# A hybrid decoder trunk: the RWKV triangular solves' copies, stores and loads on other queues and at other steps, and the last key tile's products moved

## The chip, the cores and the metric

The kernel runs on one core of a Trainium2 chip. The metric is the device time of one execution in microseconds, the median of several runs.

## The reference

Two decoder layers over 1024 positions of width 1024. Layer 0 mixes tokens by a gated linear recurrence, layer 1 by RWKV-7 time mixing; each layer also has cross-attention into 256 memory tokens and a squared-ReLU MLP. The change touches the RWKV mixer alone:

```python
xx = x_prev - x
r = (x + xx*mu[0]) @ w_rkv[0];  k = (x + xx*mu[2]) @ w_rkv[1];  v = (x + xx*mu[3]) @ w_rkv[2]
...
state = state * w_t + sa * b_t + v_t * k_t          # sa = state @ a_t; a = -kk, b = kk * a
y_t = state @ r_t                                   # 16 heads of 64, 1024 steps
```

All arrays are float32. The kernel does the recurrence in 16 chunks of 64 positions. Within a chunk the state correction needs the inverse of a unit triangular 64x64 matrix for each head and chunk.

## The kernel before

A float32 product is done as three matmuls on a high and a low part (lines 304 to 306, in `mm3`); `split` (lines 203 and 204) makes the parts, the high one on ScalarE, the low one on VectorE. Almost all tiles are 128x1024 "units" from one pool of 45 buffers. Matmul weights are loaded on SyncE's DMA queue (line 235) in the order in which they are used, a few ahead.

The program text gives the instructions a priority; a planner with an engine model then fixes the order on each engine and hands out buffers as they come free in its plan. On the chip each engine works its list in that order. `with self.behind():` pins what is emitted in it behind the last instruction emitted so far on the same engine. `self.between` holds small pieces of work, one of which is emitted after each product of three matmuls in a tile's second half.

The RWKV stage has 20 steps, counted by `aside(step)`. In steps 0 to 6 the eight 128-column tiles f of the keys are multiplied (tiles 6 and 7 together in step 6); `prep_head(f)` empties the PSUM tile (lines 1183 and 1184) and `prep_rest(f)` makes kp (line 1190), the squares sq (line 1192), b and a (lines 1193 to 1197) and stores them. `sums` and `gram` of a tile follow a step or more later (lines 1218 to 1248) and store the chunks' triangular matrices. Steps 7 to 12 multiply the receptance (tiles 0 and 1 together, then 2 to 5, then 6 and 7 together; line 1353 empties them), steps 13 to 19 the values. Two PSUM tiles of this size are in use, so a product waits until the one before the last has been emptied.

The triangular matrices of two tiles f are inverted together as solve q: `solve_load` fetches them (line 1252) and sets the result tile to the identity (lines 1253 and 1254), `solve` does 31 pairs of a multiply (line 1268) and an add (line 1270), `solve_store` makes a transposed copy (line 1280) and stores both (lines 1281 and 1282). Solves 0 to 2 run on GpSimd, solve 3 on VectorE through `self.between`. The solve inverts 32x32 halves; `merge_load` (lines 1286 to 1294), `merge` (two small products, lines 1306 and 1313) and `merge_store` (line 1320) join them for each f. The steps at which load, solve and store of solve q stand are the lists

```python
SL, SO, ST = (2, 4, 6, 9), (2, 4, 6, 9), (2, 4, 6, 12)
```

and those of the merges are ML (9 + f), ME (10 + f) and MS (11 + f).

Of the kernel before, what the change touches and what calls it, by code (L numbers as in the profile page):

```python
# [992 lines left out]

TURNS = [[f] for f in range(6)] + [[6, 7]]

SL, SO, ST = (2, 4, 6, 9), (2, 4, 6, 9), (2, 4, 6, 12)
ML, ME, MS = range(9, 17), range(10, 18), range(11, 19)
SE = [lambda nc: nc.gpsimd] * 3 + [lambda nc: nc.vector]
DA = (2, 1)
LD = 6  # L1000
POST = lambda nc: nc.vector
# [47 lines left out]
def rwkv_make_mix(self, X, i, hf, out, js=range(KT // 2)):  # L1049

    nc = self.nc

    def parts(m):
        h, l = self.split(m)
        out.extend((h[:, s], l[:, s]) for s in (slice(0, 512), slice(512, 1024)))

    ms = []
    for j in js:
        m = self.unit()
        for k in (2 * j, 2 * j + 1):  # L1060
            o = (k % 2) * 512
            mu = self.col("mu", i * 8 + k)
            nc.scalar.activation(m[:, o:o + 512], X[hf][:, k, :], AF.Copy, scale=self.omu[:, i * 8 + k:i * 8 + k + 1])
            if hf:
                nc.scalar.activation(m[:, o:o + 1], X[0][:, k, 511:512], AF.Identity, scale=mu, bias=m[:, o:o + 1])
            nc.vector.scalar_tensor_tensor(m[:, o + 1:o + 512], X[hf][:, k, :511], mu, m[:, o + 1:o + 512], ALU.mult, ALU.add)
        ms.append(m)
        if len(ms) > 1:
            parts(ms.pop(0))
    parts(ms.pop(0))  # L1070
# [31 lines left out]
def rwkv(self, X, xt, lw_wa, lw_g, post):  # L1102
    nc, I = self.nc, self.I
# [3 lines left out]
    XTd = self.dram([128, 8, 1024])  # L1107
# [3 lines left out]
    Mod = self.dram([8, 2, 32, 16, 32])  # L1111
    Ld = self.dram([4, 2, 2, 2, 16, 32, 32])
    Xd = self.dram([4, 2, 2, 2, 16, 32, 32])
    Xnd = self.dram([8, 2, 16, 32, 32])
# [9 lines left out]
    for hf in range(2):  # L1124
# [13 lines left out]
        if hf:  # L1138
            h = maps[0][2]
# [4 lines left out]
    h = maps[1][2]  # L1144
# [11 lines left out]
    dk, st_k, mg, sol, ld, sm, xts = {}, {}, {}, {}, {}, {}, {}  # L1156
# [22 lines left out]
    def prep_head(f, pk):  # L1179
        a, P, IP = dk[f]  # L1180

        at = self.unit()
        nc.scalar.activation(at, pk, AF.Copy, scale=self.nkk[:, f:f + 1])
        nc.vector.tensor_mul(IP, IP, pk)  # L1184
        dk[f] = a, P, IP, at

    def prep_rest(f):
        a, P, IP, at = dk.pop(f)
        kp = self.unit()
        nc.vector.tensor_scalar(kp, a, self.col("k_a", f), self.kam[:, f:f + 1], ALU.mult, ALU.add)  # L1190
        sq = self.unit()
        nc.scalar.activation(sq, at, AF.Square)
        nc.vector.scalar_tensor_tensor(a, a, self.col("k_k", f), IP, ALU.mult, ALU.mult)

        nc.vector.tensor_mul(ch(at)[:, :, 1:], ch(at)[:, :, 1:], ch(P)[:, :, :63])
        nc.sync.dma_start(MVd[:, f, 0, :], at)
        nc.vector.tensor_mul(kp, kp, IP)
        for h in range(2):
            nc.sync.dma_start(STd[hr[h], f, h, :], a[hr[h], :])
            nc.sync.dma_start(STd[hr[h], f, 1 - h, :], kp[hr[h], :])  # L1200
        st_k[f] = sq, a, at

    def prep(f, pk):
        prep_head(f, pk)
        if f < 6:
            prep_rest(f)
        if f == 7:
            rwkv_make_mix(self, X, 0, 0, xr[0], range(2, 4))
            gram(5)
            rwkv_make_mix(self, X, 0, 1, xr[1])  # L1210
            prep_rest(6)
            prep_rest(7)

    def sums(f):

        ps = sm[f] = self.bank()
        for tt in range(8):
            self.between.append(lambda tt=tt: mm(ps[:, tt * 2:tt * 2 + 2], st_k[f][0][:, tt * 128:tt * 128 + 128], self.ind,
                                                 start=True, stop=True))

    def gram(f):
        sq, a, at = st_k.pop(f)
        ps = sm.pop(f)
        d2 = self.sp.tile([128, 16], F32, name=self.nm("d2"), tag="d2", bufs=3)
        nc.vector.tensor_scalar(d2.rearrange("p (h t) -> p h t", h=2), ps[:, 0:16].rearrange("p (t h) -> p h t", h=2), 1e-24, None, ALU.max)
        nc.vector.reciprocal(d2, d2)
        for par in range(2):
            for h in range(2):
                nc.sync.dma_start(self.db[h * 64:h * 64 + 64, f * 16 + par * 8:f * 16 + par * 8 + 8],
                                  d2[par * 64:par * 64 + 64, h * 8:h * 8 + 8])  # L1230
        mt = self.unit()
        dv = self.db[:, f * 16:f * 16 + 16].rearrange("p (a t) -> p t a", a=2)
        for e in range(2):
            pg = self.bank()
            for c in range(8):
                s = slice(c * 64, c * 64 + 64)
                sc = slice(e * 512 + c * 64, e * 512 + c * 64 + 64)
                for h in range(2):
                    rs = slice(h * 64, h * 64 + 64)
                    mm(pg[rs, s], a[rs, sc], at[rs, sc], start=True, stop=True)  # L1240
            nc.vector.tensor_tensor(mt[:, e * 512:e * 512 + 512].rearrange("p (t a i) -> p t a i", a=2, i=64),
                                    pg.rearrange("p (t a i) -> p t a i", a=2, i=64),
                                    dv[:, e * 4:e * 4 + 4].unsqueeze(3).broadcast_to([128, 4, 2, 64]), ALU.mult)
        for h in range(2):
            for b in range(2):
                rs = slice(h * 64 + b * 32, h * 64 + b * 32 + 32)
                nc.sync.dma_start(Ld[f // 2, b, f % 2, h].rearrange("c s t -> s c t"), ch(mt)[rs, :, b * 32:b * 32 + 32])
            nc.sync.dma_start(Mod[f, h], ch(mt)[h * 64:h * 64 + 32, :, 32:64])

    def solve_load(q):  # L1250
        sol[q] = L, xt_ = [self.unit() for _ in range(2)]
        (nc.sync if q == 3 else nc.gpsimd).dma_start(L, Ld[q].rearrange("b q h c s t -> (b q h c) (s t)"))
        nc.gpsimd.memset(xt_, 0.0)
        nc.gpsimd.memset(xt_[:, ::33], 1.0)

    def solve(q):

        L, xt_ = sol[q]
        eng = SE[q](nc)
        tmp = stmp[q == 3]  # L1260
# [16 lines left out]

    def solve_store(q):
        L, xt_ = sol.pop(q)
        SE[q](nc).tensor_copy(L[0:64].rearrange("p (s j) -> p s j", j=32), xt_[0:64].rearrange("p (j s) -> p s j", s=32))  # L1280
        nc.gpsimd.dma_start(Xd[q].rearrange("b q h c s t -> (b q h c) (s t)"), xt_)
        nc.gpsimd.dma_start(Xnd[2 * q:2 * q + 2].rearrange("q h c s t -> (q h c) (s t)"), L[0:64])

    def merge_load(f):
        XT = self.unit()
        nc.gpsimd.memset(XT, 0.0)
        XN = self.unit()
        xc = ch(XT)
        for h in range(2):
            for b in range(2):  # L1290
                rs = slice(h * 64 + b * 32, h * 64 + b * 32 + 32)
                nc.gpsimd.dma_start(xc[rs, :, b * 32:b * 32 + 32], Xd[f // 2, b, f % 2, h].rearrange("c s t -> s c t"))
            nc.gpsimd.dma_start(XN[h * 64:h * 64 + 32, 0:512].rearrange("p (c t) -> p c t", t=32), Xnd[f, h].rearrange("c s t -> s c t"))
            nc.gpsimd.dma_start(XN[h * 64:h * 64 + 32, 512:1024].rearrange("p (c t) -> p c t", t=32), Mod[f, h])
        mg[f] = XN, XT

    def merge(f):
        XN, XT = mg.pop(f)
        xc = ch(XT)
        r0 = [slice(h * 64, h * 64 + 32) for h in range(2)]  # L1300
# [14 lines left out]
        for h in range(2):  # L1315
            nc.scalar.copy(xc[r0[h], :, 32:64], ps[r0[h], :].rearrange("p (c t) -> p c t", t=32))
        xts[f] = XT

    def merge_store(f):
        nc.gpsimd.dma_start(XTd[:, f, :], xts.pop(f))  # L1320

    def aside(step):

# [5 lines left out]

    self.depth, self.ahead = DA  # L1330
    decay(0)
# [15 lines left out]
    def early(f):  # L1347
        ld[f] = self.unit()
        nc.sync.dma_start(ld[f], Pd[f * 128:f * 128 + 128, :])
# [6 lines left out]
    for i, fs in enumerate([[0, 1], [2], [3], [4], [5], [6, 7]]):  # L1356
        for f in fs:
            early(f)
        if i == 5:
            self.later.append(lambda: rwkv_make_mix(self, X, 3, 0, xv[0], range(3)))  # L1360
        if i in (1, 2):
            sums(5 + i)
        self.fphase(I["b_w_rkv"][0, 0], fs, xr, evac_r, spread=i == 0)
        if i in (1, 2):
            gram(5 + i)
        aside(len(TURNS) + i)
# [201 lines left out]
    for c in range(16):  # L1568
# [4 lines left out]
        s = cst[c]  # L1573
# [113 lines left out]
```

## Time and profile before

| | |
|---|---|
| median of three runs | 3032.07 us (3031.96 to 3038.93) |
| profiled execution | 3026.98 us; span of its instructions 3025.3 us |
| TensorE busy | 2866.9 us, 95% of the span |
| VectorE, ScalarE, GpSimd busy | 1799.5, 1350.1 and 1186.1 us |
| RWKV stage, key products to the last merge | about 1400 to 1810 us of the span |

The profiled execution is one of its own, some 5 us below the median of the runs. PE is TensorE's matmuls, DVE VectorE, ACT ScalarE, POOL GpSimd, SP SyncE (it only issues DMAs). A busy share is an average: what TensorE lacks is found in the stretches in which it is not busy, and in those in which the granted clock (PEclk, 1.00 is 2.4 GHz) is below one.

### The profile page before, as it was taken

What the parts mean: (1) busy time and instruction counts of PE and PEld (TensorE: products, weight loads), DVE (VectorE), ACT (ScalarE), POOL (GpSimd) and SP (SyncE); (2) the same over time, 40 slices, a digit from 0 to 9 for tenths busy, and PEclk for the clock granted to TensorE, in tenths of its full rate; (3) what the DMA queues carried; (4) which work ended last, traced back from release to release, by engine and by line L of the source; (5) the groups of instructions that cost most, each with busy time, mean ns of one, the idle gap of its engine ahead of it and who ended that gap; (6) DMA issues with size and microseconds to landing.
All of it is one profiled execution on the core that took longest, in us unless ns stands there. A gap on an engine that the chain in (4) does not pass through costs nothing. (4 is left out here: it accounts for less than half of the span.)

```text
span 3025.3 us, 42919 instructions
## 1 busy us (share of the span) xinstructions
PE 2866.9 (95%) x16987; PEld 2382.4 (79%) x16987; DVE 1799.5 (59%) x1991; ACT 1350.1 (45%) x1939; POOL 1186.1 (39%) x1108
## 2 busy tenths in 40 slices
PE   7999999898999999989978999999999899999998
PEld 6888898786888878877866777878888678887886
DVE  5576552547355688767673726884344644568776
ACT  5464342535454543447340534443244545454332
POOL 2000100015666754441587424652001466667442
PEclk9999999998999999999988999999999999999999
DMA  8213261122544564332646889852312244455443
GB/s 260 73 42 101 80 213 55 57 84 70 169 154 154 216 213 148 115 126 86 168 113 198 223 241 230 183 134 84 105 43 90 71 152 153 153 205 197 161 139 119
DMA packets 370857, 421.93 MB, mean 139 GB/s; under 512 B 78960, under 2 KB 280928, under 8 KB 370656
## 3 DMA queue, kind: packets, MB, share of 16 engines
q1 hardware_dynamic: 356128, 371.85, 40.9%
q0 software_dynamic: 14064, 46.75, 4.3%
q8 instruction: 134, 2.20, 0.3%
q14 instruction: 67, 0.55, 0.1%
q10 hardware_dynamic: 464, 0.59, 0.1%
HBM read 284.31 MB, written 134.74 MB: 139 GB/s over the span
## 5 line engine op out<-in xcount | busy, mean ns | idle before, releaser
L204 DVE TENSOR_TENSOR u<-u,u 128x1024 fp32r<-128x1024 f32 (+1 forms) x518 | 816.7, 1604 | 344.2 <-ACT u L203 328.6
L304 PE MATMUL p<-u,u 128*128 128x512 f32 (+1 forms) x1920 | 717.9, 377 | 44.8 <-DVE u L1184 16.8
L203 ACT CAST u<-u 128x1024 fp32r<-128x1024 f32 (+1 forms) x550 | 542.9, 1024 | 484.5 <-PE q L305 159.5
L305 PE MATMUL p<-u,u 128*128 128x512 f32 (+1 forms) x1920 | 719.9, 375 | 9.4 <-DVE u L204 9.4
L306 PE MATMUL p<-u,u 128*128 128x512 f32 (+1 forms) x1920 | 716.5, 374 | 3.8 <-DVE u L204 3.7
L304 PE MATMUL q<-u,u 128*128 128x512 f32 (+1 forms) x1632 | 641.8, 394 | 25.4 <-ACT u L203 10.7
L305 PE MATMUL q<-u,u 128*128 128x512 f32 (+1 forms) x1632 | 637.8, 392 | 7.0 <-DVE u L204 7.0
L306 PE MATMUL q<-u,u 128*128 128x512 f32 (+1 forms) x1632 | 633.1, 391 | 0.0
L304 PEld LDWEIGHTS p<-u,u 128*128 128x128 f32 x1920 | 367.6, 192 | 112.9 <-issue 23.2
L315 POOL TENSOR_SCALAR s<-s 128x1 f32<-128x1 f32 x98 | 37.1, 378 | 994.3 <-ACT u L313 993.3
L305 PEld LDWEIGHTS p<-u,u 128*128 128x128 f32 x1920 | 368.4, 192 | 74.1 <-DVE u L204 13.5
L306 PEld LDWEIGHTS p<-u,u 128*128 128x128 f32 x1920 | 368.2, 192 | 68.2 <-DVE u L204 5.8
L304 PEld LDWEIGHTS q<-u,u 128*128 128x128 f32 (+1 forms) x1632 | 307.9, 189 | 96.7 <-ACT u L203 12.8
L305 PEld LDWEIGHTS q<-u,u 128*128 128x128 f32 (+1 forms) x1632 | 308.4, 189 | 73.1 <-DVE u L204 9.3
L306 PEld LDWEIGHTS q<-u,u 128*128 128x128 f32 (+1 forms) x1632 | 307.8, 189 | 64.1
L431 POOL TENSOR_TENSOR u<-u,u 128x1024 f32<-128x1024 f32 x64 | 179.1, 2820 | 86.4 <-DVE u L204 80.2
L976 DVE TENSOR_TENSOR z<-z,q 128x512 f32<-128x512 f32 x192 | 128.8, 680 | 90.6 <-PE q L306 90.3
L204 POOL TENSOR_TENSOR u<-u,u 128x1024 fp32r<-128x1024 f32 x32 | 94.0, 2937 | 164.9 <-ACT u L203 99.2
L411 POOL TENSOR_TENSOR u<-u,u 128x512 f32<-128x512 f32 x96 | 151.0, 1582 | 2.9
L927 POOL TENSOR_TENSOR u<-u,u 128x512 f32<-128x512 f32 x32 | 47.0, 1469 | 165.2 <-ACT u L916 159.1
L304 PE MATMUL q<-z,u 128*128 128x512 f32 x256 | 102.4, 400 | 7.0 <-DVE u L611 7.0
L204 DVE TENSOR_TENSOR u<-p,u 128x1024 fp32r<-128x1024 f32 x32 | 38.9, 1221 | 108.6 <-ACT u L203 108.6
(260 smaller groups left out, 3533.7 us busy)
## 6 DMA issues: line engine op xcount, KB each, us to landing
u<-d SPq DMA_DIRECT2D x198, 512.0 KB, 4.7
d<-u SPq DMA_DIRECT2D x101, 512.0 KB, 3.3
d<-u POOLq DMA_DIRECT2D x76, 512.0 KB, 4.1
d<-u SPq DMA_DIRECT2D x128, 256.0 KB, 3.6
u<-in_m_w_up SPq DMA_DIRECT2D x64, 512.0 KB, 5.4
u<-in_m_w_down SPq DMA_DIRECT2D x64, 512.0 KB, 5.1
u<-in_c_w_kv SPq DMA_DIRECT2D x32, 512.0 KB, 6.5
u<-d SPq DMA_DIRECT2D x56, 256.0 KB, 6.2
```

The lines of the kernel that those rows point to most:

```text
L203: self.nc.scalar.copy(hv, src)
L204: (eng or self.nc.vector).tensor_tensor(lv, src, hv, ALU.subtract)
L304: mm(o, ah, bh, start=first, stop=False, **kw)
L305: mm(o, ah, bl, start=False, stop=False, **kw)
L306: mm(o, al, bh, start=False, stop=last, **kw)
L315: nc.gpsimd.tensor_scalar(v, ss, 1.0 / n, eps, ALU.mult, ALU.add)
L411: sub = lambda o, x, y: nc.gpsimd.tensor_tensor(o, x, y, ALU.subtract)
L431: self.nc.gpsimd.tensor_tensor(f[o][i], f[x][i], f[y][i], ALU.subtract)
L927: tt(s1, r21, r22, ALU.add)
L976: nc.vector.tensor_add(to_, to_, o)
```

## The change

The lists of steps change: solve 1 is loaded and run at step 5 instead of 4, solve 2 at 8 instead of 6; the stores move from (2, 4, 6, 12) to (5, 8, 12, 13). In `solve_load` the memsets run on the engine of the solve, which differs for solve 3 alone (VectorE instead of GpSimd). In `solve_store` the copy runs on ScalarE instead of the solve's engine, and both stores go to SyncE's queue instead of GpSimd's. For the tiles f below 4 the merge's loads and its store go to SyncE's queue and its memset to VectorE. `prep_rest(7)` is emitted after the first receptance pair instead of directly before it.

```diff
-SL, SO, ST = (2, 4, 6, 9), (2, 4, 6, 9), (2, 4, 6, 12)
+SL, SO, ST = (2, 5, 8, 9), (2, 5, 8, 9), (5, 8, 12, 13)
 SE = [lambda nc: nc.gpsimd] * 3 + [lambda nc: nc.vector]
+MQ = lambda nc, f: nc.sync if f < 4 else nc.gpsimd
@@ prep(f, pk), f == 7
             prep_rest(6)
-            prep_rest(7)
@@ solve_load(q)
-        nc.gpsimd.memset(xt_, 0.0)
-        nc.gpsimd.memset(xt_[:, ::33], 1.0)
+        SE[q](nc).memset(xt_, 0.0)
+        SE[q](nc).memset(xt_[:, ::33], 1.0)
@@ solve_store(q)
-        SE[q](nc).tensor_copy(L[0:64].rearrange("p (s j) -> p s j", j=32), xt_[0:64].rearrange("p (j s) -> p j s", s=32))
-        nc.gpsimd.dma_start(Xd[q].rearrange("b q h c s t -> (b q h c) (s t)"), xt_)
-        nc.gpsimd.dma_start(Xnd[2 * q:2 * q + 2].rearrange("q h c s t -> (q h c) (s t)"), L[0:64])
+        nc.scalar.copy(L[0:64].rearrange("p (s j) -> p s j", j=32), xt_[0:64].rearrange("p (j s) -> p j s", s=32))
+        nc.sync.dma_start(Xd[q].rearrange("b q h c s t -> (b q h c) (s t)"), xt_)
+        nc.sync.dma_start(Xnd[2 * q:2 * q + 2].rearrange("q h c s t -> (q h c) (s t)"), L[0:64])
@@ merge_load(f)
+        dma = MQ(nc, f).dma_start
         XT = self.unit()
-        nc.gpsimd.memset(XT, 0.0)
+        (nc.vector if f < 4 else nc.gpsimd).memset(XT, 0.0)
...
-                nc.gpsimd.dma_start(xc[rs, :, b * 32:b * 32 + 32], Xd[f // 2, b, f % 2, h].rearrange("c s t -> s c t"))
+                dma(xc[rs, :, b * 32:b * 32 + 32], Xd[f // 2, b, f % 2, h].rearrange("c s t -> s c t"))
...
@@ merge_store(f)
-        nc.gpsimd.dma_start(XTd[:, f, :], xts.pop(f))
+        MQ(nc, f).dma_start(XTd[:, f, :], xts.pop(f))
@@ receptance loop, i the turn
         self.fphase(I["b_w_rkv"][0, 0], fs, xr, evac_r, spread=i == 0)
+        if i == 0:
+            prep_rest(7)
```

## Rows read from the trace of the kernel before

**Rows 1.** Busy time by stretch, 1500 to 1720: stretch, length, engines, PEclk, DMA

```profile
1580.00:1600.00 20.00, 16.61 (x135) 14.34 (x134) 13.39 (x12) 0.51 (x1) 16.53 (x19) 0.83 0.80 247
...
1640.00:1660.00 20.00, 8.27 (x86) 6.00 (x84) 9.48 (x23) 0.00 (x0) 14.07 (x26) 0.74 0.52 147
...
sum 220.00, PE 179.85 PEld 144.23 DVE 131.68 ACT 80.37 POOL 159.18; mean PE 16.35 PEld 13.11 DVE 11.97 ACT 7.31 POOL 14.47
```

**Rows 2.** TensorE's waits, 1500 to 1720: total, times, longest, us

```profile
PE p L304 <- DVE u L1184: 16.8, 2, 11.6
PE p L304 <- DVE u L1270: 10.9, 1, 10.9
...
PE p L304 <- DVE u L1353: 3.4, 1, 3.4
```

**Rows 3.** VectorE's timeline: start, duration, instruction, idle before and its releaser

```profile
1529.56 0.81 DVE L1190 TENSOR_SCALAR u<-u,colt,kam 128x1024 f32<-128x1024 f32 x1 [10.86 <-POOL u L1254]
1530.29 1.21 DVE L1184 TENSOR_TENSOR u<-u,p 128x1024 f32<-128x1024 f32 x1
...
1579.47 1.95 DVE L1190 TENSOR_SCALAR u<-u,colt,kam 128x1024 f32<-128x1024 f32 x2
...
1590.97 2.34 DVE L1353 TENSOR_TENSOR u<-u,p 128x1024 f32<-128x1024 f32 x2
...
1650.04 0.19 DVE L1268 TENSOR_TENSOR w<-u,u 128x31 f32<-128x31 f32 x1 [29.55 <-POOL u L1254]
1650.14 1.21 DVE L1353 TENSOR_TENSOR u<-u,p 128x1024 f32<-128x1024 f32 x1
...
1683.43 1.21 DVE L1353 TENSOR_TENSOR u<-u,p 128x1024 f32<-128x1024 f32 x1
```

**Rows 4.** ScalarE's timeline

```profile
1531.12 1.06 ACT L1192 ACTIVATE u<-u 128x1024 f32<-128x1024 f32 x1 [11.60 <-DMA d<-u]
...
1635.47 1.05 ACT L203 CAST u<-u 128x1024 fp32r<-128x1024 f32 x1 [1.97 <-DMA u<-in_b_w_rkv]
```

**Rows 5.** GpSimd's timeline

```profile
1524.63 1.89 POOL L1280 COPY u<-u 64x1024 f32<-64x1024 f32 x1
...
1527.07 0.56 POOL L1282 DMA_DIRECT2D d<-u  x1
...
1532.42 0.50 POOL L1268 TENSOR_TENSOR w<-u,u 128x31 f32<-128x31 f32 x1 [2.92 <-DMA u<-d]
...
1592.77 1.99 POOL L1280 COPY u<-u 64x1024 f32<-64x1024 f32 x1
...
1606.72 0.23 POOL L1268 TENSOR_TENSOR w<-u,u 128x31 f32<-128x31 f32 x1 [9.06 <-DMA u<-d]
...
1645.85 1.88 POOL L1280 COPY u<-u 64x1024 f32<-64x1024 f32 x1
```

**Rows 6.** SyncE's issues

```profile
1612.85 1.06 SPq L1247 DMA_DIRECT2D d<-u  x2
...
1625.67 0.34 SPq L1252 DMA_DIRECT2D u<-d  x1
...
1627.75 0.38 SPq L235 DMA_DIRECT2D u<-in_b_w_rkv  x1
```

**Rows 7.** TensorE's timeline around the end of its longest wait

```profile
1531.55 0.79 PE L304 MATMUL p<-u,u 128*128 128x512 f32 x1 [11.60 <-DVE u L1184]
...
1532.57 0.63 PE L306 MATMUL p<-u,u 128*128 128x512 f32 x1
1533.00 0.63 PE L304 MATMUL p<-u,u 128*128 128x512 f32 x1
...
1535.84 0.40 PE L305 MATMUL p<-u,u 128*128 128x512 f32 x1
1536.07 0.40 PE L306 MATMUL p<-u,u 128*128 128x512 f32 x1
```

**Rows 8.** Busy time by stretch, 1720 to 1820, all five of 20 us

```profile
sum 100.00, PE 100.00 PEld 78.06 DVE 31.72 ACT 37.65 POOL 25.37; mean PE 20.00 PEld 15.61 DVE 6.34 ACT 7.53 POOL 5.07
```

More of the change, by code (lines that the diff above doesn't have):

```diff
@@ L1279, in solve_store @@
         L, xt_ = sol.pop(q)
-        SE[q](nc).tensor_copy(L[0:64].rearrange("p (s j) -> p s j", j=32), xt_[0:64].rearrange("p (j s) -> p s j", s=32))
-        nc.gpsimd.dma_start(Xd[q].rearrange("b q h c s t -> (b q h c) (s t)"), xt_)
-        nc.gpsimd.dma_start(Xnd[2 * q:2 * q + 2].rearrange("q h c s t -> (q h c) (s t)"), L[0:64])
+        nc.scalar.copy(L[0:64].rearrange("p (s j) -> p s j", j=32), xt_[0:64].rearrange("p (j s) -> p s j", s=32))
+        nc.sync.dma_start(Xd[q].rearrange("b q h c s t -> (b q h c) (s t)"), xt_)
+        nc.sync.dma_start(Xnd[2 * q:2 * q + 2].rearrange("q h c s t -> (q h c) (s t)"), L[0:64])
     def merge_load(f):
+        dma = MQ(nc, f).dma_start
         XT = self.unit()
-        nc.gpsimd.memset(XT, 0.0)
+        (nc.vector if f < 4 else nc.gpsimd).memset(XT, 0.0)
         XN = self.unit()
@@ L1291, in merge_load @@
                 rs = slice(h * 64 + b * 32, h * 64 + b * 32 + 32)
-                nc.gpsimd.dma_start(xc[rs, :, b * 32:b * 32 + 32], Xd[f // 2, b, f % 2, h].rearrange("c s t -> s c t"))
-            nc.gpsimd.dma_start(XN[h * 64:h * 64 + 32, 0:512].rearrange("p (c t) -> p c t", t=32), Xnd[f, h].rearrange("c s t -> s c t"))
-            nc.gpsimd.dma_start(XN[h * 64:h * 64 + 32, 512:1024].rearrange("p (c t) -> p c t", t=32), Mod[f, h])
+                dma(xc[rs, :, b * 32:b * 32 + 32], Xd[f // 2, b, f % 2, h].rearrange("c s t -> s c t"))
+            dma(XN[h * 64:h * 64 + 32, 0:512].rearrange("p (c t) -> p c t", t=32), Xnd[f, h].rearrange("c s t -> s c t"))
+            dma(XN[h * 64:h * 64 + 32, 512:1024].rearrange("p (c t) -> p c t", t=32), Mod[f, h])
         mg[f] = XN, XT
```

## The prediction

> **What bounds the kernel now.** I read the page first: TensorE is busy for most of the span, so only stretches in which it stands idle, or runs at the lower clock, can give time back; everything else is cover. The busy times by stretch come next [rows 1]. Over the 220 us from 1500 to 1720 us, where the key products, the first receptance products and three of the four solves lie, TensorE works 179.85 us, so 40.15 us are idle. The same rows show its granted clock: 0.83 and 0.74 in the two stretches with idle time that stand there. Two levels are meant, 2.4 GHz and 1.2 GHz, mixed within a stretch. Third, TensorE's own waits in the same window [rows 2]: 16.8 us in two waits for line 1184 (the multiply that empties a key product's PSUM tile), 10.9 us for line 1270 (the last add of a solve step that ran on VectorE), 3.4 us for line 1353 (the multiply that empties a receptance product's tile). These 31.1 us are four of the waits; the rest are below 2 us each. Last, the timelines of the engines that let TensorE wait, to see what they themselves waited for.
>
> In the first wait, line 1184 [rows 3] starts at 1530.29, right after line 1190 of tile 5's `prep_rest`, which had stood for 10.86 us. ScalarE shows the same halt [rows 4]: its line 1192 for the same tile, at 1531.12, had waited 11.60 us for a store to DRAM. That store is the solve's: GpSimd finished solve 0 and began its copy at 1524.63 and issued line 1282 at 1527.07 [rows 5]. VectorE's halt is put down to a GpSimd memset, but line 1190 does not touch that tile; with line 1192 beside it I read both as waits for the two work buffers that solve 0 held until its stores landed. So the key products stood still because kp and sq were given solve 0's buffers.
>
> In the third wait, VectorE stood 29.55 us before the first multiply of solve 3 at 1650.04 [rows 3], for line 1254: the memset of solve 3's result tile, on GpSimd behind all of solve 2, whose copy began at 1645.85 [rows 5]. Line 1353 of receptance tile 4 was queued on VectorE behind that multiply, and TensorE needed its PSUM tile. Before line 1353 of the first pair, at 1590.97, VectorE did the two `prep_rest` of tiles 6 and 7, from 1579.47 on [rows 3].
>
> **The memset of solve 3 goes to VectorE.** GpSimd's 29.55 us are no longer in front of solve 3. What is late next is the load of its L tile, issued on SyncE at 1625.67 [rows 6]. The nearest load of that kind is solve 2's on GpSimd: from its copy at 1592.77 the tile was there at 1606.72 [rows 5], of which 3.1 us are the copy and two issues that stood ahead, so under 11 us. Solve 3 can then start by about 1637, before TensorE runs out of work at 1640.6 (the 10.9 us wait ended at 1651.5, just after line 1353). I take the whole wait away: 10.9 us. A restart also costs clock. After the 11.60 us wait, matmuls start 0.43 us apart (1532.57 and 1533.00) and later 0.23 us apart (1535.84 and 1536.07) [rows 7]; about nine are slow, from 1531.55 on, so 9 x 0.20 = 1.8 us. Together 12.7 us. Bounds: nothing, if the L load or a buffer is as late as the memset was, to 12.7.
>
> **Solve 0's copy and stores move to step 5.** They stand on ScalarE and SyncE behind that step's last instructions there, so behind tile 5's line 1192. This tile's kp and sq cannot then be given solve 0's buffers, since these come free later on the same engine. They must take others; the nearest that come free are those of tile 4's gram, which TensorE finished at 1531.55 - 11.60 = 1519.95 [rows 7]. Line 1190 would go at about 1520 instead of 1529.56: 9.6 us, and with the restart 11.4 us. Bounds: nothing (the buffers given instead are as late) to 13.4 (the wait of 11.6 with the restart). I take 11.4. The second wait for line 1184, 16.8 - 11.6 = 5.2 us, I leave: VectorE and ScalarE work through the mixes in front of it, and this chain shifts with the first wait. Its bounds are nothing and 5.2 + 1.8 = 7.0 us.
>
> **`prep_rest(7)` moves behind the first receptance pair.** Two `prep_rest` take VectorE 1590.97 - 1579.47 = 11.5 us, one 5.75. With one less ahead, line 1353 comes 5.75 us earlier than 1590.97, more than the 3.4 us that TensorE waited. With the restart (the granted clock of this stretch was 0.83 [rows 1]) 5.2 us; bounds nothing and 5.2. Its five stores on SyncE move with it; its sums and gram are two steps later, so nothing waits for them at once.
>
> **What the moved work costs.** The four copies on ScalarE: the nearest row is line 1192, 128x1024, 1.06 us [rows 4]; GpSimd took 1.89 [rows 5]. In between, and 4 x 1.06 = 4.2 us in all on an engine busy 80.37 of 220 us [rows 1], so hidden unless it waits for its solve. The memsets (solve 3's, and four of the merge loads) are bounded by nothing and by a 128x1024 multiply's 1.21 us on the same engine [rows 3], so 5 x 1.21 = 6 us at most on VectorE, covered by the 29.55 us that it stood. SyncE gets 8 solve stores, 32 merge loads and 4 merge stores: at 0.53 us each (1.06 for two of line 1247 [rows 6]) 23 us of issuing. Spread over steps 5 to 13 that is nothing for SyncE itself; the weight loads behind it come later by up to 4 us per step (8 x 0.53), and the one at 1627.75 was split at 1635.47 while TensorE had work until 1640.6 [rows 4, 6], so there are some 5 us of cover. If that cover is gone, each step costs up to 4 us.
>
> A wait is added where ScalarE and SyncE stand at a copy whose solve is not done. Solve 1: GpSimd is freed of 3 us of copy and issues, so it would run from about 1529.4, take its 60.3 us (1532.42 to 1592.77 [rows 5]) and end near 1590. Step 8's place on SyncE is at line 1247's stores, 1612.85 [rows 6] less the 11.4 and 5.2 us saved before it: 1596. Six us to spare. Solve 2 would then start near 1601. It took 39.1 us (1606.72 to 1645.85) while VectorE stood still; solve 1 took 60.3 us beside a working VectorE. So it ends between 1640 and 1661. Step 12's place is behind the last line 1353, 1683.43 + 1.21 less 29.3: 1655. ScalarE would stand there up to 6 us with the value mixes queued behind it, and TensorE waits for these. Because solve 3 now runs on VectorE at the same time, I take a value near the upper end: 4 us. Bounds 0 and 6 + 1.8.
>
> The Trainium skill says of this (SBUF — State Buffer, section "SBUF: two separate sides") that VectorE and GpSimd share one pair of ports under an exclusive lock, and that a VectorE instruction with two SBUF inputs takes it against a GpSimd instruction that reads SBUF. The rows agree in direction, 60.3 against 39.1 us; by that rule alone solve 2 and solve 3 side by side would each be slowed, and the 4 us would be the whole 6 to 8.
>
> **Sum.** 12.7 + 11.4 + 5.2 - 4 = 25.3 us. The profiled execution took 3026.98 us (span 3025.3), so 3001.7 by it. The median of the runs, 3032.07, lies 5.1 us above that execution, so 3006.8; I give 3007. The 100 us behind this stretch have TensorE busy without a gap [rows 8], so they should shift as they are. About 0.3% (9 us) is what a measurement of this kernel can tell from no change.
>
> **Rivals.**
>
> *Only the VectorE halt goes* (buffers come free no earlier, so the first wait remains): 12.7 + 5.2 - 4 = 13.9 us, 3018. For it: all waits for buffers in that stretch come from one pool, and solve 0 now holds two of them for longer. Against: the two it held are excluded as the cause. Chance 0.2. Without line 1353's part too it is 3023, the edge of no change.
>
> *Waits only change their name.* The halt for GpSimd's memset is replaced by ScalarE and SyncE standing at steps 8 and 12, for as long as solve 2 is late. If solves 1 and 2 together end one contended solve's excess (60.3 - 39.1 = 21 us) after step 12's place, that comes back as one gap of TensorE with its restart: 3032 - 29 + 21 + 2 = 3026. For it: GpSimd runs both without a break. Against: by the times above solve 2 is at most 6 us late. Chance 0.15 that it ends within 0.3%.
>
> *Slower: weight loads starve.* Two of the work buffers are held three steps longer by solve 0, and two more by solve 1 up to step 8. If it is the weights that go without, each tile's weight is loaded when the tile is due. From issue to split that is 7.7 us (1627.75 to 1635.47 [rows 4, 6]) and with VectorE's half and the restart about 10 us for each of tiles 6, 7, 0, 1, 2: 50 us against 25.3 gained, 3057. From the fourth exposed weight on (40 against 25.3, with the bound of 9) it decides. For it: line 1192 did wait for a buffer, so the pool is empty there. Against: SyncE had weights ahead through 1640. Chance 0.15.
>
> *All four waits go*, the second for line 1184 too, and no copy stands: 12.7 + 13.4 + 7.0 + 5.2 = 38.3 us, 2994. Chance 0.1.
>
> My forecast has 0.4. Faster than 0.3%: 0.4 + 0.1 + 0.2 = 0.7; same 0.15; slower 0.15. The range runs from 2989, a little under the best sum, to 3036, so that of the slower case nearly all is left out; the forecast's own range is 2997 to 3014.
>
> **What the profile afterwards should show.** No wait of VectorE for GpSimd ahead of line 1268, and TensorE without a stop near 1640: step one right. Line 1192 of tile 5 not waiting for a store: step two right. Line 1353's first pair directly behind one `prep_rest`. ScalarE's new line 1280 standing less than 6 us in each of its four places, and solve 2 on GpSimd between 39 and 60 us. The forecast is wrong if line 1280 or the stores on SyncE stand for ten or more, if weights (line 203 behind a load of the products' weights) stop TensorE in steps 5 to 9, or if the two matmul waits reappear under other names.

## The result and the profile after

The changed kernel takes 3014.12 us (median of four runs, 3011.39 to 3015.65), the kernel before 3032.6 on the same chip: ratio 0.9933, interval 0.9916 to 0.9951, so 18.5 us less. Predicted were 3007 and a gain of 25. The profiled execution took 3011.39 us (span 3009.7, 15.6 below that of before); sums below go by it. Lines 1184, 1190, 1192 and 1353 are now 1185, 1191, 1193 and 1354; lines 1384, 1306 and 1394 are 1387, 1307 and 1397.

First TensorE's waits, 1500 to 1720 us, the window of [rows 1, 2] (total, times, longest, in us):

```profile
PE q L1397 <- ACT u L1387: 12.4, 1, 12.4
PE p L305 <- DVE u L204: 3.9, 6, 0.8
PE p L304 <- DVE u L1185: 2.8, 1, 2.8
PE p L304 <- DVE u L1354: 2.8, 2, 1.9
PE q L1307 <- DMA u<-d: 2.6, 3, 2.0
```

Two of the waits of [rows 2] are almost gone: 16.8 us for the key products' multiply are 2.8, and the 10.9 us for line 1270 no longer appear. The 3.4 us for the receptance's multiply are 2.8. At the top stands a stop of 12.4 us that was 1.7 before: line 1397, which transposes a finished value tile, waits for line 1387, ScalarE's copy of that tile out of PSUM. Now the busy times by stretch of the changed kernel (columns as in [rows 1]):

```profile
1660.00:1680.00 20.00, 18.12 (x122) 13.33 (x116) 19.62 (x39) 17.06 (x28) 3.62 (x2) 1.00 0.96 276
1680.00:1700.00 20.00, 7.60 (x25) 5.44 (x25) 10.14 (x15) 3.58 (x5) 6.01 (x9) 0.66 0.99 184
```

In the second stretch TensorE works 7.60 of 20 us and the granted clock is 0.66, a mixture of 2.4 and 1.2 GHz: the stop, and the slow matmuls behind it. The DMA engines are busy throughout, 0.96 and 0.99. The timelines say what is late. ScalarE's (start, duration, instruction, idle before and its releaser):

```profile
1510.01 1.06 ACT L1193 ACTIVATE u<-u 128x1024 f32<-128x1024 f32 x1
1527.44 2.07 ACT L1280 COPY u<-u 64x1024 f32<-64x1024 f32 x1 [16.37 <-POOL u L1270]
...
1591.28 2.08 ACT L1280 COPY u<-u 64x1024 f32<-64x1024 f32 x1 [21.68 <-POOL u L1270]
...
1656.28 2.12 ACT L1280 COPY u<-u 64x1024 f32<-64x1024 f32 x1
...
1692.52 1.04 ACT L203 CAST u<-u 128x1024 fp32r<-128x1024 f32 x1 [13.02 <-DMA u<-in_b_w_rkv]
1693.59 1.01 ACT L1387 COPY u<-p 128x1024 f32<-128x1024 f32 x1
```

The last two rows are the new stop. ScalarE stood 13.02 us at line 203, the split of the fourth value tile's weight (tile 3); line 1387, the copy of tile 0 that TensorE waited for, was next in its list. (The weights of tiles 0 and 1 are taken together, and taking one splits the weight two further on, so tile 3's split stands ahead of tile 0's copy.) Line 203 waited for the load, which SyncE's timeline shows:

```profile
1639.09 2.24 SPq L235 DMA_DIRECT2D u<-in_b_w_rkv  x2
1654.00 5.46 SPq L1355 DMA_DIRECT2D d<-u  x2
1659.55 0.38 SPq L1281 DMA_DIRECT2D d<-u  x1
...
1677.37 0.39 SPq L235 DMA_DIRECT2D u<-in_b_w_rkv  x1
```

The weights of value tiles 1 and 2 are issued at 1639.09. Tile 3's, the twentieth of this matrix's 24 loads (keys and receptance have eight each), follows only at 1677.37; the expectations below take it for tile 2's. SyncE first stands 12.6 us at line 1355, the stores of the last receptance tiles, until 1654.00; then come these, solve 2's stores, one merge's eight loads, another merge's store and the early loads of later stages. The weight is ready for its split 15.1 us after its issue. In the kernel before, the same load was slow too, and TensorE's wait behind it was 1.7 us:

```profile
1696.07 0.39 SPq L235 DMA_DIRECT2D u<-in_b_w_rkv  x1
```

```profile
1711.44 1.04 ACT L203 CAST u<-u 128x1024 fp32r<-128x1024 f32 x1 [2.21 <-DMA u<-in_b_w_rkv]
```

It took 15.4 us there. So the growth of the stop by 10.7 us is not a slower transfer. Counted from the end of the last multiply that empties a receptance product (1684.64 before, 1659.09 after), the weight is issued 18.3 us later instead of 11.4 and split 33.4 us later instead of 26.8, while TensorE comes to the stop 23.2 us later instead of 27.2: 6.6 us are a later weight, 4.0 an earlier TensorE.

VectorE and GpSimd complete the picture:

```profile
1604.99 0.91 DVE L1253 MEMSET u<- 128x1024 f32 x1 [0.16 <-issue]
...
1613.14 0.59 DVE L1268 TENSOR_TENSOR w<-u,u 128x31 f32<-128x31 f32 x1 [4.91 <-DMA u<-d]
...
1628.48 0.61 DVE L1268 TENSOR_TENSOR w<-u,u 128x192 f32<-128x192 f32 x1
```

```profile
1597.06 0.23 POOL L1268 TENSOR_TENSOR w<-u,u 128x31 f32<-128x31 f32 x1 [3.44 <-DMA u<-d]
...
1637.82 0.40 POOL L1270 TENSOR_TENSOR u<-u,w 128x31 f32<-128x31 f32 x1
```

Solve 3 starts on VectorE at 1613.14 instead of 1650.04 [rows 3]; solve 2 runs beside it and ends at 1638.2, 18 us before its copy on ScalarE at 1656.28.

### The profile page after: what moved, and what is told of

The parts are those of the page before. It is cut to its first block, busy times and chain, and to the rows that moved or that the text cites. A ratio compares the mean times of both kernels' runs of the same rounds, so it can differ in the third digit from the quotient of the medians.

```text
span 3009.7 us, 42878 instructions
## 1 busy us (share of the span) xinstructions
PE 2867.0 (95%) x16987; PEld 2382.3 (79%) x16987; DVE 1811.5 (60%) x1996; ACT 1357.9 (45%) x1943; POOL 1152.8 (38%) x1055
## 5 line engine op out<-in xcount | busy, mean ns | idle before, releaser
L411 POOL TENSOR_TENSOR u<-u,u 128x512 f32<-128x512 f32 x96 | 150.8, 1580 | 2.9
L611 DVE SCALAR_TENSOR_TENSOR u<-p,s,u 128x1024 f32<-128x1024 f32 x24 | 30.8, 1284 | 122.1 <-ACT u L203 77.9
```

Source lines behind the costliest of these rows:

```text
L411: sub = lambda o, x, y: nc.gpsimd.tensor_tensor(o, x, y, ALU.subtract)
L611: nc.vector.scalar_tensor_tensor(o, src, r, gb, ALU.mult, ALU.mult)
```

## The experiments

Twelve kernels ran, in three groups. The reference runs of before gave 3031.81 us for the first four kernels, 3031.66 for e5 to e8 and 3033.02 for e9 to e12. Ratios are to these.

**The memset alone** (e1), on the kernel before:

```diff
-        nc.gpsimd.memset(xt_, 0.0)
-        nc.gpsimd.memset(xt_[:, ::33], 1.0)
+        SE[q](nc).memset(xt_, 0.0)
+        SE[q](nc).memset(xt_[:, ::33], 1.0)
```

> The kernel before with only the memsets of solve 3's result tile moved from GpSimd to VectorE. Theory (my first step): VectorE no longer stands 29.55 us, TensorE's 10.9 us stop near 1640 us goes with its restart, 12.7 us: 3020 against 3032.6. Rival: something else is as late as the memset was (the load of L, a buffer): the stop stays under another name, 3030 or more. Second rival: solve 3 beside solve 2 slows both, the value products stop later instead, 3025 or more.

Measured: 3031.79 us, 1.0002 (0.9993 to 1.0012). Nothing. TensorE's waits in the same window:

```profile
PE p L304 <- DVE u L1184: 16.4, 2, 11.6
PE q L1306 <- DMA u<-d: 12.6, 1, 12.6
PE p L304 <- DVE u L1353: 3.4, 1, 3.4
```

The 10.9 us are gone and 12.6 us stand in their place, at the first merge product. Its loads are on GpSimd's queue behind solve 2: the solve's copy is at 1648.80, the loads at 1652.78 to 1654.65, and TensorE, which works its own list in order, reaches the product and stands until 1656.63.

**`prep_rest(7)` alone** (e2), on the kernel before:

```diff
@@ prep(f, pk), f == 7
-            prep_rest(7)
@@ receptance loop
         self.fphase(I["b_w_rkv"][0, 0], fs, xr, evac_r, spread=i == 0)
+        if i == 0:
+            prep_rest(7)
```

> The kernel before with only the rest of key tile 7 moved behind the first receptance pair. Theory (my third step): the 3.4 us wait for line 1353 and its restart go, 5.2 us: 3027.5. Rival: the planner's order around it hides it or the kept inputs of tile 7 block two buffers more, no change within 3 us: 3030 to 3036.

Measured: 3027.89 us, 0.9984 (0.9974 to 0.9993), 3.9 us less. The wait for the receptance's multiply fell from 3.4 to 0.4 us, while the wait for the solve's add near 1640 is 1.4 us longer in this execution:

```profile
PE p L304 <- DVE u L1184: 16.8, 2, 11.3
PE p L304 <- DVE u L1269: 12.3, 1, 12.3
...
PE p L304 <- DVE u L1352: 0.4, 1, 0.4
```

**Steps, copies and stores alone** (e3), on the kernel before: the new lists SL, SO and ST, the copies on ScalarE, the stores on SyncE; memsets, merges and `prep_rest(7)` as before.

```diff
-SL, SO, ST = (2, 4, 6, 9), (2, 4, 6, 9), (2, 4, 6, 12)
+SL, SO, ST = (2, 5, 8, 9), (2, 5, 8, 9), (5, 8, 12, 13)
@@ solve_store(q)
-        SE[q](nc).tensor_copy(...)
-        nc.gpsimd.dma_start(...)
+        nc.scalar.copy(...)
+        nc.sync.dma_start(...)
```

> The kernel before with the new lists of steps, the copies on ScalarE and the solves' stores on SyncE; the memsets, the merges' queue and the rest of key tile 7 stay as before. Theory (my second step): the two waits for line 1184 shrink from 16.8 to about 3 us as in the changed kernel, but solve 3's memset still stands behind solve 2, so the stop near 1640 stays: 13 us gained, 3019. Rival: the waits for line 1184 shrink only together with the other parts: 3030. Second rival: solve 2 at step 8 ends later, and solve 3's memset behind it costs more than the 10.9 us before: 3025 or more.

Measured: 3019.36 us, 0.9957 (0.9942 to 0.9972), 12.4 us less.

```profile
PE p L304 <- DVE u L1270: 11.1, 1, 11.1
PE q L1394 <- ACT u L1384: 7.9, 1, 7.9
PE p L304 <- DVE u L1353: 5.2, 1, 5.2
PE p L304 <- DVE u L1184: 2.9, 1, 2.9
```

The waits for the key products' multiply are down here, with none of the rest of the change. The value stop of the changed kernel has begun: 7.9 us where before had 1.7, though no merge load is on SyncE.

**The changed kernel with its merges on GpSimd again** (e4):

```diff
-MQ = lambda nc, f: nc.sync if f < 4 else nc.gpsimd
+MQ = lambda nc, f: nc.gpsimd
-        (nc.vector if f < 4 else nc.gpsimd).memset(XT, 0.0)
+        nc.gpsimd.memset(XT, 0.0)
```

> The changed kernel with the merges' loads, stores and memsets of all tiles on GpSimd as before the change. In the changed kernel TensorE stops 12.4 us near 1682 us; behind it stands a load of a value weight, issued at 1677.37, after 11 merge issues that took SyncE from 1659.55 to 1667.02. Theory A, SyncE's issuing makes the stop: it shrinks by about 7 us to 5, and the time falls to 3007. Theory B, the load takes 15 us to land because the DMA engines are full, whichever queue the merges use: the stop stays above 10 us, 3014 within 3. Theory C, the merges behind solve 2 on GpSimd now come too late for TensorE: 3019 or more.

Measured: 3013.63 us, 0.9935 (0.9918 to 0.9951), like the changed kernel.

```profile
PE q L1307 <- DMA u<-d: 15.1, 1, 15.1
PE q L1397 <- ACT u L1387: 6.4, 1, 6.4
```

By the medians a stop of 15.1 us at the merge is worth nothing here. The next one, for the value weight, is 6.0 us shorter behind it, and all waits of the window add up to 28.2 us against 25.4 in the changed kernel. The weight was issued at 1681.66 with the merge loads on another queue, and still took 12.1 us to its split.

**The value tiles' copy on VectorE** (e5), in the changed kernel, for tiles 0 and 1:

```diff
-        nc.scalar.copy(vt, p)
+        (nc.vector.tensor_copy if f < 2 else nc.scalar.copy)(vt, p)
```

> The changed kernel with the copies of the first two value tiles out of PSUM on VectorE instead of ScalarE. ScalarE's order (line 203, the split of a weight that has not landed, ahead of line 1387) holds TensorE's transposes in the 12.4 us stop. Theory C, the order on ScalarE makes the stop: transposes and the bonus product of two tiles go during it, about 4 us of TensorE's work, so 4 us or more come back: 3010 or less. Theory B, the weight's landing sets the end of the stop and what ScalarE has behind the split (line 1412) holds the rest: 3014 within 2.

Measured: 3016.72 us, 0.9946 (0.993 to 0.9963): no gain. TensorE's first wait only has another name:

```profile
PE q L1397 <- DVE u L1387: 14.1, 1, 14.1
```

So the place of the copy on ScalarE alone is not what costs; VectorE's half of the same split waits for the same weight.

**Early loads later** (e6): the early loads of value tile 2 (and so on for each turn) are emitted behind the products of the turn before, not ahead of them, so that fewer loads stand ahead of the weight.

```diff
+        self.fphase(I["b_w_rkv"][0, 2], fs, xv, evac_v, spread=i == 0)
         for f in turns[i + 1] if i < 6 else []:
             early(f)
-        self.fphase(I["b_w_rkv"][0, 2], fs, xv, evac_v, spread=i == 0)
```

> The changed kernel with the three loads for value tile 2 (lines 1421 and 1423) emitted behind the products of tiles 0 and 1 instead of ahead of them, so ahead of the weight's load on SyncE stand three loads and 1 MB less. Theory B (the weight takes 12 to 15 us to land behind what was issued before it): it lands about 4 us earlier, 3010. Theory A (SyncE's issue time alone): 1.8 us earlier, 3012. Theory C (ScalarE's order, whatever the load does): as B, since the split comes earlier by the same.

Measured: 3012.11 us, 0.9933 (0.9918 to 0.9948). The weight is issued at 1674.65 instead of 1677.37, but split at 1690.80, 16.2 us later; the stop is 10.0 us.

**One more weight ahead** (e7): at the last receptance pair the loader is let one weight further ahead, in the changed kernel.

```diff
@@ receptance loop, the turn with i == 5
+            self.ahead += 1
```

> The changed kernel with one more weight loaded ahead from the last receptance pair on, so the weight of value tile 2 is issued with the two before it, near 1640 instead of 1677, ahead of the loads that fill the DMA engines. Theory B: the 12.4 us stop shrinks to under 3 us, with its restart 11 us come back: 3003. Rival: the weight of tile 3 is late instead, or the buffer that the early weight holds is missing elsewhere: a stop of 8 us or more under the same or another name, 3011 or more.

Measured: 3000.44 us (2999.68 to 3001.43), 0.9894 (0.9879 to 0.9909): 31 us below the kernel before and, by the two ratios, 0.0039 x 3032 = 11.8 us below the changed one. TensorE's wait, SyncE's issue and ScalarE's copy:

```profile
PE q L1398 <- ACT u L1388: 0.4, 1, 0.4
```

```profile
1640.75 5.71 SPq L235 DMA_DIRECT2D u<-in_b_w_rkv  x3
```

```profile
1683.38 1.02 ACT L1388 COPY u<-p 128x1024 f32<-128x1024 f32 x1 [1.15 <-PE p L306]
```

Three weights instead of two go out before the burst of stores and loads. The copy then waits for TensorE alone, and the 12.4 us are 0.4.

**Memset and merges without the new steps** (e8): the changed kernel with the steps and `solve_store` of before, and `prep_rest(7)` back in its place.

```diff
-SL, SO, ST = (2, 5, 8, 9), (2, 5, 8, 9), (5, 8, 12, 13)
+SL, SO, ST = (2, 4, 6, 9), (2, 4, 6, 9), (2, 4, 6, 12)
@@ solve_store(q)
-        nc.scalar.copy(...)
-        nc.sync.dma_start(...)
+        SE[q](nc).tensor_copy(...)
+        nc.gpsimd.dma_start(...)
```

> The kernel before with solve 3's memsets on VectorE and the merges' loads, stores and memsets of tiles 0 to 3 on SyncE and VectorE; steps, copies and solve stores as before. With the memset alone TensorE stopped 12.6 us for a merge's load on GpSimd behind solve 2. Theory: the two parts are one, both stops go, 10.9 us and the restart come back: 3020. Rival: as in the changed kernel the value weight is then late by as much, since it is issued by SyncE behind the merges: a stop of 6 us or more at line 1394, 3026 or more.

Measured: 3041.78 us, 1.0033 (1.0021 to 1.0044): 10 us slower than before. SyncE's own waits from 1660 to 1710, and its timeline:

```profile
SPq L1294 <- DVE u L1288: 9.4, 1, 9.4
```

```profile
1690.36 2.53 SPq L1294 DMA_DIRECT2D u<-d  x4
...
1704.38 0.39 SPq L235 DMA_DIRECT2D u<-in_b_w_rkv  x1
```

A merge's memset now stands on VectorE behind the whole of solve 3 and its copy (line 1288 at 1689.42). SyncE waits 9.4 us at the loads into that tile, and the value weight queued behind them goes out at 1704.38. TensorE's stop for the value tile's copy is 11.5 us, and a wait of 7.7 us for a split is new beside it (TensorE's waits, 1500 to 1760):

```profile
PE q L1396 <- ACT u L1386: 11.5, 1, 11.5
PE p L304 <- ACT u L203: 7.7, 1, 7.7
```

**The weight ahead, on the kernel before** (e9):

```diff
@@ receptance loop, the turn with i == 5
+            self.ahead += 1
```

> The kernel before with one more weight loaded ahead from the last receptance pair on, nothing else. If the value weight is late only because the work ahead of it was shortened (theory), there is little to win here, 1.7 us of wait at line 1394: 3029 to 3032. Rival: the weight ahead is worth its 11 us by itself, whatever the solves do: 3021 or less.

Measured: 3028.33 us, 0.9988 (0.9978 to 0.9997), 0.0012 x 3033 = 3.6 us less. It fills a stop that is small before (1.7 us); the waits of 16.8 and 9.7 us remain.

**The merges on GpSimd with the weight ahead** (e10), in the changed kernel: the diffs of e4 and e7 together,

```diff
-MQ = lambda nc, f: nc.sync if f < 4 else nc.gpsimd
+MQ = lambda nc, f: nc.gpsimd
-        (nc.vector if f < 4 else nc.gpsimd).memset(XT, 0.0)
+        nc.gpsimd.memset(XT, 0.0)
+            self.ahead += 1
```

> The changed kernel with the merges of all tiles on GpSimd again, and one more weight ahead. With the weight late, moving the merges back cost nothing (3013.6 against 3014.1), though a 15.1 us wait for a merge's load came back. Theory: the late weight covered it; with the weight ahead the wait shows in full, 12 us or more above the 3000.4 of the changed kernel with the weight ahead: 3012 or more. Rival: the merges' queue is worth nothing in either case: 3003 or less.

Measured: 3005.02 us, 0.9909 (0.9894 to 0.9923), 4.9 us above e11, its neighbour on the chip, where 12 or more were expected. The merge stop is there in full, 15.1 us against 3.0 in e7, but all waits of the window add up to only 8.0 us more than in e7 (22.2 against 14.2): 4.1 us are given back there by shorter other waits. Where the rest is given back was not settled.

**Two weights ahead** (e11), in the changed kernel at the place of e7:

```diff
+            self.ahead += 2
```

> The changed kernel with two more weights ahead. Theory: the one late weight was the whole stop, the second is not needed: 3000 within 3. Rival: a second weight's buffers are missing elsewhere: 3006 or more; or tile 3's weight was late too: 2996 or less.

Measured: 3000.08 us, 0.9893 (0.9877 to 0.991), the same as e7. One is enough.

**e7 with solve 3's memsets back on GpSimd** (e12):

```diff
-        SE[q](nc).memset(xt_, 0.0)
-        SE[q](nc).memset(xt_[:, ::33], 1.0)
+        nc.gpsimd.memset(xt_, 0.0)
+        nc.gpsimd.memset(xt_[:, ::33], 1.0)
```

> The changed kernel with one more weight ahead and solve 3's memsets back on GpSimd, behind solve 2. Theory: VectorE stands for the memset again, as before the change, and TensorE with it: my first term of 12.7 us shows at last, 3013. Rival: it is worth nothing here too, 3003 or less.

Measured: 3018.18 us, 0.9952 (0.9937 to 0.9967), 18.1 us above e11. TensorE's waits in 1500 to 1720, then VectorE's in 1600 to 1660:

```profile
PE p L304 <- DVE u L1354: 17.3, 3, 14.2
```

```profile
DVE w L1268 <- POOL u L1254: 29.7, 1, 29.7
```

## Why the prediction was right or wrong

The direction was right, and of what was to be seen afterwards all but the short standing of line 1280 came; the gain was 18.5 us instead of 25.3, which puts the median 0.1 us above the forecast's own range of 2997 to 3014. By terms:

| term | predicted | measured |
|---|---|---|
| solve 3's memset on VectorE | 12.7 | 0 alone (e1); 18.1 with the rest of the change and the weight in time (e11, e12) |
| solve 0's copy and stores at step 5 | 11.4 | 12.4 (e3: all new steps, copies and stores) |
| `prep_rest(7)` | 5.2 | 3.9 alone (e2) |
| ScalarE standing at step 12 | -4 | 0: no wait there |
| value weight late | 0 | -12.4 of stop, 1.7 of which stood before; 11.8 of time (e7) |

How far the changed kernel is ahead of the one before shows where the forecast was lost. At the last multiply that empties a receptance product it is 25.6 us ahead (1683.43 [rows 3] against 1657.88); the forecast had 29.3 there. At the transposes behind the new stop it is 18.9 (1713.57 against 1694.65), at the next value tile's copy 16.6 (1716.85 against 1700.23), at the end 15.6. The loss is at the value weight and in the slow clock behind it. The rows (VectorE's in the changed kernel, then TensorE's before and after):

```profile
1657.88 1.21 DVE L1354 TENSOR_TENSOR u<-u,p 128x1024 f32<-128x1024 f32 x1
```

```profile
1713.57 1.09 PE L1394 MATMUL q<-ident,u 128*128 128x128 f32 x8 [1.72 <-ACT u L1384]
```

```profile
1694.65 1.97 PE L1397 MATMUL q<-ident,u 128*128 128x128 f32 x8 [12.40 <-ACT u L1387]
```

That the total came as near as it did is in part luck: the 4 us for ScalarE that were taken off and never came, and the 2.4 us of the second wait for line 1184 that were not counted, make up for 6.4 us of what was lost there.

**One step that failed** is in the working of the memset: "What is late next is the load of its L tile". The memset did stop solve 3, VectorE's 29.55 us did go, and so did TensorE's 10.9. But the load was not the next thing that was late. With the merges on GpSimd it is the merge product (e1, 12.6 us). With the merges on SyncE and the old steps it is SyncE itself, behind a merge's memset (e8). In the changed kernel the wait near 1640 is gone, but what is late next is the fourth value tile's weight. I looked for what was late for solve 3, not for the next entry in TensorE's list. The lower bound of this term, nothing, was what the single edit gave; I took the upper one.

**The second step that failed** is "Spread over steps 5 to 13 that is nothing for SyncE itself" with its 5 us of cover. The cover was measured at a weight of step 9 and taken for all. At the fourth value tile's weight there is none: TensorE had waited 1.7 us for it already before the change. The price at that one place was 12.4 us, three times the 4 us per step that I gave. The rival in which weight loads starve was thus right in kind, at one tile instead of five. Its cause was not the one it named: no buffer was missing, since e7 has the same buffers held and loads the weight without trouble. It was issued late for a transfer that is slow there, in the kernel before (15.4 us) as after: issued at 1674.65 (e6), 1677.37 (changed) and 1681.66 (e4), it was split at 1690.80, 1692.52 and 1693.78. Between these kernels an issue 7.0 us earlier bought 3.0, and a queue without merge loads (e4) left 12.1 us to the split, where the weight of [rows 4, 6] took 7.7. Only an issue from before the burst (e7) takes the stop away.

**Solve 0's stores** went as forecast. Tile 5's line 1193 runs at 1510.01 without a wait, where line 1192 had waited 11.60 us for the store [rows 4]; e3 shows 12.4 us against 11.4. The second wait for the same line, which I left at 5.2 us with a bound of nothing to 7.0, went down too: one wait of 2.8 remains of the two. So the likeliest rival against this step, that only VectorE's halt goes, is refuted; e3 and e1 show the reverse of it. That the number agrees so well is partly chance: e3 moves the copies and stores of all four solves and the steps of two, its waits for line 1184 are 13.9 us shorter, and its value stop is 6.2 us longer. No run moves solve 0 alone.

**`prep_rest(7)`** was right in kind: alone it takes its wait to 0.4 us. In the changed kernel TensorE still waits 1.9 us at that pair. It comes there earlier, which may be why; no run tests that.

**ScalarE's copies** stood 16.4 and 21.7 us at steps 5 and 8. I had written that ten would make the forecast wrong. The second cost nothing: TensorE works 20.00 of the 20 us from 1580 to 1600. Behind the first, VectorE stood too, and TensorE's remaining wait for line 1185 comes at the end of that chain (VectorE's timeline, then TensorE's):

```profile
1530.49 2.36 DVE L204 TENSOR_TENSOR u<-u,u 128x1024 fp32r<-128x1024 f32 x2 [13.19 <-ACT u L203]
```

```profile
1539.65 0.64 PE L304 MATMUL p<-u,u 128*128 128x512 f32 x1 [2.79 <-DVE u L1185]
```

So it cost at most these 2.8 us and a restart; that it did cost them is read from the order, and no run tests it. The test should have named the waiter, not the wait. At step 12 there was no wait: solve 2 took 41.2 us (1597.06 to 1638.2), near the low end of 39 to 60 and not near the upper one that I chose. The Trainium skill (SBUF — State Buffer, "SBUF: two separate sides") has VectorE and GpSimd exclude each other on a shared pair of ports. The trace agrees in direction: solve 2's multiplies average 623 ns in the changed kernel, 566 in the kernel before, where VectorE mostly stands still, and 869 beside VectorE's 128x1024 work (solve 1, after). But the price for solve 2 was 2 us and not the 6 to 8 of that paragraph, and its three longest multiplies (2.48, 1.38 and 1.14 us, at 1606.17, 1629.62 and 1632.85) stand beside VectorE's 128x1024 instructions, not beside solve 3's small ones.

**The clock**: behind the stop of 12.4 us the granted clock is 0.50 (1.2 GHz) from 1695 to 1700 and 0.98 in the next 5 us. Half of the 5.3 us from 1694.65 on, 2.7 us, is lost, more than the 1.8 to 2 that I gave a restart. The 1.8 us of the predicted terms were not measured by themselves.

The sum by parts: 12.4 (e3) + 3.9 (e2) = 16.3 us, which leaves 2.2 of the 18.5 for the memset and the merges together. Once the weight comes in time the memset is worth 18.1 (e12) and the merges' move 4.9 (e10). The effects don't add: memset and merges without the new steps lose 10 us (e8).

**Open**: what the late weight waits for on its way, the transfers issued ahead of it or engines busy with other queues' (the mean DMA share while the load was on its way was 0.92 and 0.98 for the two of 7.7 us and 1.09 and 1.11 for those of 15.4 and 15.1, which does not tell the two apart); what the move of solve 0 is worth by itself; and where e10 gives back most of its merge stop.

## What to carry to other kernels

After taking a stall out, read the next entries in the list of the engine that was freed, and of the queues on which their operands come: here the gain went into the merge's loads in one version and into a weight load in another, and only the load issued ahead of the burst made it time. A DMA that waits for its tile holds up what stands behind it in its issuing queue (9.4 us in e8), so a prefetch belongs in front of stores and loads that can stand. Price a new wait by who waits behind it: 21.7 us on ScalarE cost nothing, 13.0 us at another place cost 12.4.

## What the runs showed of the hardware

- The solve's transposed copy of 64x1024 float32 takes 2.01 to 2.12 us on ScalarE (changed kernel), above my bounds of 1.06 to 1.89 us, 1.88 to 2.00 on GpSimd (before, e1) and 1.02 on VectorE (e8, 1688.24), although ScalarE's plain 128x1024 pass takes 1.06.
- A 128x1024 memset takes 0.91 us on VectorE and 0.97 on GpSimd, so in this kernel where it stands matters only by what is queued around it.
- A solve on VectorE is slower beside one on GpSimd: the 128x192 multiply takes VectorE 0.61 us beside GpSimd's solve (row at 1628.48) and 0.36 us in e8 (1683.14), where GpSimd is idle. GpSimd's own 128x192 multiply takes 0.55 us beside solve 3 (1628.32) and 0.53 before it starts (1603.59).
- A weight load takes 7.7 us to its split in two places (1627.75 before, with a mean DMA share of 0.92 on its way; 1639.09 after, split at 1646.74, with 0.98), and 12 to 16 us behind the burst of stores and loads, in the kernel before as in the changed one (1.09 and 1.11 on its way).
